# The first sum of a unit's weight blocks, made by an accumulating transfer in place of a VectorE addition, in the input projection of a hybrid retention and recurrence layer

## The chip, the cores and the metric

The kernel runs on one core of a Trainium2 chip. The metric is the device time of one execution in microseconds (us), less is better. Engines: TensorE (PE, matmuls), VectorE (DVE), ScalarE (ACT), GpSimd (POOL) and SyncE (SP, which issues most of the DMA transfers).

## The reference, cut to what matters

One layer over 1024 positions and 1024 channels, all in float32. The stage of this case is the combined input projection, whose 8192 columns are q and k, v, the swish gate, the two branches of the recurrence and the two merge gates.

```
h = rms_norm(x, norm1_w[l])
proj = h @ w_in[l]
q, k, v, g_ret, x_lru, y_lru, gate_ret, gate_lru = jnp.split(proj, SPLIT_POINTS, axis=-1)
...
x = x + mix @ w_out[l]
h = rms_norm(x, norm2_w[l])
up = h @ ffn_w_up[l]
...
```

## The kernel before, in words

**Tiles and products.** Every large product is taken by a fast scheme of the Strassen-Winograd kind: a unit of 256 output columns and 1024 positions is made of seven products of blocks in place of eight. A unit's weights (the A side) are four blocks of 128x512 float32, A11, A12, A21 and A22, 256 KB each, loaded from DRAM into tiles of the pool `w` (22 tiles). From them come seven operands, in the order `PRODS` (line 528): A11, S1 = A21 + A22, S2 = S1 - A11, A12, S3 = A21 - A11, A22, S4 = A12 - S2. Each operand is split into a rounded high part and a rest, which are two more `w` tiles: a cast on ScalarE (line 597) and a subtraction on VectorE (line 598). PE then runs 12 matmuls of 128x128 by 128x512 to a product (line 848): four slices of the contraction, with three of the four combinations of high and rest. The B side (positions) is split once and kept in the pool `u`.

**Who calls what.** `loads()` (line 635) issues a unit's block loads on SyncE in the job's own order (line 649). `prep_fast()` (line 673) makes the operands: S1 by a VectorE addition into a new tile (line 683), S2 in that same tile (line 686), S4 in the same tile again (line 689), S3 in the tile of A11 (line 692). `mm_fast()` (line 826) issues the products. `pump()` (line 727) lets preparation run up to seven finished operands ahead of PE (`NBLK`) and loads up to six blocks ahead of preparation (`AHEAD`).

**The input projection.** 24 units go through this (`add`, line 1763). The order is `SEQ` (line 549): merge gates, the recurrence's branches, and four retention heads of two units each, with the recurrence, the retention and the sums for later stages running beside them as generators that `advance()` takes in turn. v's columns are made ahead of it by a routine of their own, `values()`. The other stages that use the same helpers (both branch outputs, the output projection, the feed-forward part) have 48 more units.

**What sets the order.** The program is built twice. `Plan` reads the first build, gives every instruction a duration and every transfer a time to landing from its own table, ranks all instructions by when they are due, and forms an order for each engine. 150 drafts, made by random shifts around the waits that its own model shows, are tried and the best is kept; the second build is held to it. So each engine's queue is fixed, and a changed instruction anywhere lets all of it be drawn anew. Engines meet by semaphores only. SyncE, GpSimd and ScalarE each issue their transfers in their fixed order, and an instruction that waits holds up all that stands behind it on its engine.

**GpSimd before.** In this stage it copies the rotary tables (lines 1182 to 1185, eight transfers) and raises the variances of the retention's groups to -1/2 (line 1410, eight times, 128x4). Later it issues the stores to `ff_d` (line 1941).

Of the kernel before, what the change touches and what calls it, by code (L numbers as in the profile page):

```python
# [16 lines left out]
ALU = mybir.AluOpType  # L17
# [73 lines left out]
IN_RATE = 1.5  # L91
# [436 lines left out]
PRODS = ("A11", "S1", "S2", "A12", "S3", "A22", "S4")  # L528
# [25 lines left out]
def tile_trunk_layer(ctx, tc, x, xt, front, positions, params, consts, normf, w_in, w_v, w_ro, w_lo,  # L554
                     w_out, w_up, w_dn, w_gate, out):
    nc = tc.nc
    V, S, G, PE, SY = nc.vector, nc.scalar, nc.gpsimd, nc.tensor, nc.sync
# [36 lines left out]
    def split(src, get=get):  # L594

        hi, lo = get(F32R), get(F32R)
        S.copy(hi, src)  # L597
        V.tensor_sub(lo, src, hi.bitcast(F32))  # L598
        return hi, lo
# [10 lines left out]
    class Job:  # L610
        def __init__(self, src, op, emit, post=None, fast=False, last=False, drop12=False,
                     pre=None, fetch=None, order=None, ready=None, by=None, rate=RATE, mate=False,
                     prods=PRODS, stage=None, halves=()):
            self.pre, self.ready, self.by, self.rate = pre, ready, by, rate
            self.stage, self.halves = stage, halves
            self.mate, self.prods = mate, prods
            self.order = order or (("A11", "A21", "A22", "A12") if fast else ORD_T)
            self.fetch, self.got = fetch, {}
            self.src, self.op, self.emit, self.post = src, op, emit, post
            self.fast, self.last, self.drop12 = fast, last, drop12  # L620
            self.raw, self.blk = {}, {}
# [13 lines left out]
    def loads():  # L635
        i = 0
        while True:
            while i >= len(queue):
                yield None
            group = queue[i:i + 1 + queue[i].mate]  # L640
            while group[0].stage and not state["open"]:
                yield None
            for nm in () if group[0].stage else group[0].order:
                m, kh = int(nm[1]) - 1, int(nm[2]) - 1
                for jb in group:
                    while jb.ready is not None and not jb.ready(m, kh):
                        yield None
                    t = W.get()
                    SY.dma_start(t, jb.src(m, kh))
                    jb.raw[nm] = t  # L650
                    state["raws"] += 1
                    yield True
            i += len(group)

    def raw(jb, nm):
        while nm not in jb.raw:
            if next(state["load"]) is None:
                yield None
        return jb.raw[nm]

    def done(jb, *names):
        for nm in names:
            W.put(jb.raw[nm], late=SOONER)
            state["raws"] -= 1
# [7 lines left out]

    def prep_fast(jb):
        uses = {"A11": {"A11", "S2", "S3"}, "A21": {"S1", "S3"}, "A22": {"S1", "A22"}, "A12": {"A12", "S4"}}
        s = None
        for nm in PREP.get(jb.prods, jb.prods):
            for r in uses:
                if nm in uses[r]:
                    yield from raw(jb, r)
            r = jb.raw  # L680
            if nm == "S1":
                src = s = W.get()
                V.tensor_add(s, r["A21"], r["A22"])  # L683
            elif nm == "S2":
                src = s
                V.tensor_sub(s, s, r["A11"])  # L686
            elif nm == "S4":
                src = s
                V.tensor_sub(s, r["A12"], s)  # L689
            elif nm == "S3":  # L690
                src = r["A11"] if uses["A11"] == {"S3"} else W.get()
                V.tensor_sub(src, r["A21"], r["A11"])  # L692
            else:
                src = r[nm]
            jb.blk[nm] = split(src, W.get)
            state["blocks"] += 1
            if nm == "S4" or nm == "S3" and src is not r["A11"]:
                W.put(src, late=SOONER)
            for k, u in uses.items():
                if nm in u:  # L700
                    u.remove(nm)
                    if not u:
                        done(jb, k)
            yield True

    def preps():
        i = 0
        while True:
# [14 lines left out]
            i += len(group)  # L723

    state["load"], state["prep"] = loads(), preps()

    def pump(force=None):
# [226 lines left out]
    def pair_src(w, i):  # L954
        return lambda m, kh: w[i, 2 * m + kh]
# [101 lines left out]
    h1 = {}  # L1057
# [703 lines left out]
    jobs = []  # L1761

    def add(i, emit, post=None):
        jobs.append(Job(pair_src(w_in, i), h1, emit, post, fast=True, rate=IN_RATE))

    gates = [(w, n) for n in range(4) for w in range(2)]

    def add_gate():
        w, n = gates.pop(0)
        add(16 + 4 * w + n, emit_gate(w, n))  # L1770

    for what in SEQ.split():
        if what == "v":
            jobs.append(Job(None, h1, None, stage=values))
        elif what == "g":
            add_gate()
        elif what[0] == "y":
            n = int(what[1])
            add(2 * n + 1, emit_y(n))
        elif what[0] == "x":  # L1780
            n = int(what[1])
            add(2 * n, emit_to(xl, None, True), lambda n=n: lru_block(n, dict(xl)))
        else:
            hd = int(what[1])
            base = 8 + 2 * hd

            def head(hd=hd):
                mine = dict(qk)
                return chain(rotary_head(hd, mine), retention_head(hd, mine))
            add(base, emit_to(qk), head)  # L1790
            add(base + 1, emit_to(gg, AF.Silu, True), lambda hd=hd: chain(
                ret_out(hd, dict(gg)), *(four_sums(*(og_d, to_d) if hd > 1 else (w_out, tw_d), 2 * (hd % 2) + j)
                                         for j in range(2))))
# [312 lines left out]
    def down_post(g, t):  # L2106
        def fn():
# [3 lines left out]
            if g == 1 and t == 3:  # L2111
# [5 lines left out]
                 prods=ENDING if (g, t) == (2, 3) else PRODS,  # L2117
                 halves=(slice(0, TH // 2), slice(TH // 2, TH)) if (g, t) == (2, 3) else (),
# [72 lines left out]
```

## Time and profile before

| | us |
|---|---|
| median of 3 runs | 1567.7 (1567.51 to 1568.17) |
| the profiled execution | 1566.78 |
| its span, first to last instruction | 1565.0 |
| PE busy in the span | 1557.1 |
| VectorE, ScalarE, GpSimd busy | 1343.9, 952.5, 61.0 |

The columns of an instruction group are: line, engine, operation, output<-inputs by tile names without buffer numbers, shapes, xcount | busy us, mean ns of one | the engine's idle time just before them, and what ended it. A row of waits reads: who waited for whom, us in total, times, longest. A row of the timeline reads: start, duration, engine, line, operation, tiles; in brackets the idle time before it. "q" behind an engine's name is its sequencer, which issues the DMAs. A matmul's mean of 391 ns is longer than the distance of two starts, since matmuls are pipelined.

### The profile page before, as it was taken

To read this page: it belongs to the slowest core of one execution; us is meant where nothing else is said; L and a number is where in the kernel's file an instruction comes from. 1 tells how busy PE (TensorE), PEld (TensorE's weight loads), DVE (VectorE), ACT (ScalarE), POOL (GpSimd) and SP (SyncE) were. 2 spreads that over 40 slices of the span, in tenths; PEclk is the share of its full clock that TensorE was granted. 3 is DMA by queue.
4 is the path that set the end of the run, shared out by engine and by line. 5 is a ranking of instruction groups with operands and counts; after the bars stand their busy time and mean duration, and the time that the engine had idled before them with its cause. 6 is when DMAs were issued, how large, how long until landed. Compare 5 with 4: busy or idle time off the path is not lost.

```text
span 1565.0 us, 21570 instructions
## 1 busy us (share of the span) xinstructions
PE 1557.1 (99%) x7057; PEld 1290.7 (82%) x7057; DVE 1343.9 (86%) x2397; ACT 952.5 (61%) x1675; POOL 61.0 (4%) x81
## 2 busy tenths in 40 slices
PE   9999999999999999999999999999999999999998
PEld 7888888888888888888888888888888888888887
DVE  8999988998899988999998899777777778887875
ACT  8558766766568777855456665455454547554653
POOL 0001000000000000000000001000000000000000
PEclk9999999999999999999999999999999999999999
DMA  9344334454364346875995336444444476777752
GB/s 328 121 139 130 115 129 124 140 187 155 114 203 142 101 135 186 266 276 174 315 315 173 106 115 223 141 135 142 134 138 144 146 239 196 250 266 256 265 187 80
DMA packets 157713, 278.97 MB, mean 178 GB/s; under 512 B 17048, under 2 KB 29728, under 8 KB 157600
## 3 DMA queue, kind: packets, MB, share of 16 engines
q1 hardware_dynamic: 152080, 261.79, 51.3%
q0 software_dynamic: 4224, 13.64, 2.7%
q10 hardware_dynamic: 1296, 2.17, 0.4%
q8 instruction: 55, 0.90, 0.2%
q14 instruction: 58, 0.48, 0.1%
HBM read 192.59 MB, written 83.89 MB: 177 GB/s over the span
## 4 chain that ended last, share of the span: by engine, by line
PE 93%; DMA 3%; DVE 2%; ACT 1%; issue 1%; SPq 0%; POOLq 0%; POOL 0%; DVEq 0%; ACTq 0%
PE g L848 81%; PE g L1606 5%; PE a L1257 3%; DMA w<-mix_d 1%; PE a L1382 1%; PE a L1380 1%; DMA u<-tw_d 1%; PE a L1392 1%; DVE w L598 0%; PE a L1884 0%; PE a L1372 0%; PE a L1451 0%; DMA w<-w_lo 0%; DMA sg_d<-u 0%; DVE u L598 0%
## 5 line engine op out<-in xcount | busy, mean ns | idle before, releaser
L848 PE MATMUL g<-u,w 128*128 128x512 f32 x6060 | 1412.6, 391 | 0.0
L848 PEld LDWEIGHTS g<-u,w 128*128 128x128 f32 x6060 | 1129.7, 188 | 229.0
L597 ACT CAST w<-w 128x512 fp32r<-128x512 f32 x519 | 319.0, 621 | 334.4 <-PE g L848 240.3
L598 DVE TENSOR_TENSOR w<-w,w 128x512 fp32r<-128x512 f32 x519 | 352.9, 684 | 84.4 <-ACT w L597 81.0
L597 ACT CAST u<-u 128x512 fp32r<-128x512 f32 x253 | 151.2, 619 | 60.6 <-DVE u L1239 7.5
L598 DVE TENSOR_TENSOR u<-u,u 128x512 fp32r<-128x512 f32 x253 | 166.7, 682 | 4.3 <-ACT u L597 4.0
L900 ACT COPY u<-g 128x512 f32<-128x512 f32 x148 | 86.4, 583 | 61.3 <-PE g L848 58.4
L877 DVE TENSOR_TENSOR u<-g,u 128x512 f32<-128x512 f32 x146 | 100.1, 686 | 22.1 <-PE g L848 16.8
L1936 DVE SCALAR_TENSOR_TENSOR u<-u,par,u 128x511 f32<-128x511 f32 (+1 forms) x96 | 71.6, 746 | 12.8 <-ACT u L1933 12.2
L1606 PE MATMUL g<-w,u 128*128 128x512 f32 x252 | 58.7, 389 | 0.0
L1606 PEld LDWEIGHTS g<-w,u 128*128 128x128 f32 x252 | 47.2, 188 | 9.9
L1941 POOL DMA_DIRECT2D ff_d<-u x48 | 36.2, 754 | 444.6 <-DVE u L1940 434.2
L683 DVE TENSOR_TENSOR w<-w,w 128x512 f32<-128x512 f32 x72 | 49.2, 683 | 2.7 <-DMA w<-ff_d 1.4
L897 ACT COPY g<-g 128x512 f32<-128x512 f32 x70 | 40.4, 577 | 17.8 <-PE g L848 17.6
L1257 PE MATMUL a<-u,u 128*128 128x512 f32 x192 | 50.4, 390 | 0.5 <-ACT u L597 0.5
L686 DVE TENSOR_TENSOR w<-w,w 128x512 f32<-128x512 f32 x72 | 49.3, 684 | 0.7
L689 DVE TENSOR_TENSOR w<-w,w 128x512 f32<-128x512 f32 x72 | 49.2, 683 | 0.3 <-DMA w<-w_lo 0.2
L692 DVE TENSOR_TENSOR w<-w,w 128x512 f32<-128x512 f32 x72 | 49.2, 683 | 0.4
L1933 ACT ACTIVATE u<-u,par 128x512 f32<-128x512 f32 x48 | 39.1, 816 | 7.8 <-DVE u L877 7.0
L1257 PEld LDWEIGHTS a<-u,u 128*128 128x128 f32 x192 | 35.9, 188 | 8.6 <-ACT u L597 1.3
L871 DVE TENSOR_TENSOR u<-u,u 128x512 f32<-128x512 f32 x34 | 23.2, 687 | 20.5 <-ACT u L900 20.4
L1940 DVE TENSOR_TENSOR u<-u,u 128x512 f32<-128x512 f32 x48 | 32.9, 687 | 5.4 <-ACT u L1939 5.4
(216 smaller groups left out, 1158.8 us busy)
## 6 DMA issues: line engine op xcount, KB each, us to landing
w<-w_in SPq DMA_DIRECT2D x96, 256.0 KB, 2.8
w<-w_up SPq DMA_DIRECT2D x96, 256.0 KB, 2.7
u<-w_dn SPq DMA_DIRECT2D x84, 256.0 KB, 3.2
u<-x_d SPq DMA_DIRECT2D x52, 256.0 KB, 4.4
x_d<-u SPq DMA_DIRECT2D x48, 256.0 KB, 3.6
ff_d<-u POOLq DMA_DIRECT2D x48, 256.0 KB, 2.9
td_d<-u SPq DMA_DIRECT2D x48, 256.0 KB, 3.0
u<-td_d SPq DMA_DIRECT2D x48, 256.0 KB, 4.5
```

The costliest lines, as they stand in the source:

```text
L597: S.copy(hi, src)
L598: V.tensor_sub(lo, src, hi.bitcast(F32))
L683: V.tensor_add(s, r["A21"], r["A22"])
L686: V.tensor_sub(s, s, r["A11"])
L689: V.tensor_sub(s, r["A12"], s)
L692: V.tensor_sub(src, r["A21"], r["A11"])
L848: PE.matmul(bank[:, s], w[a][:, c], need(op, (SETS[nm], j))[b][:, s], start=first and n == 0, stop=n == 11, skip_group_check=True)
L877: V.tensor_add(u, bank, u)
L900: S.copy(u, bank)
L1257: PE.matmul(ps, wg[g][a][:, cs], xs[k][b], start=q == 0, stop=q == 5)
L1606: PE.matmul(bank, o[p][:, c], w[q], start=first and j == n == 0, stop=j == 3 and n == 2, skip_group_check=True)
L1936: V.scalar_tensor_tensor(c[:, s:], src[:, :TH - s], w, c[:, s:], ALU.mult, ALU.add)
```

## The change

In the 24 units of the input projection the load order gets a fifth entry, S1. For it the block A21 is loaded into a `w` tile by SyncE, and then GpSimd issues a transfer of A22 from DRAM that adds onto that tile. That tile is S1; the VectorE addition is gone. A21 and A22 are loaded once more, for S3 and for A22 itself. The order of a unit's loads is A11, S1, A12, A21, A22 in place of A11, A21, A22, A12. The tile of S1 is now one that a load filled, and it is given back with the other loaded blocks. The other stages keep the addition.

```
+            if summed:
+                self.order = "A11", "S1", "A12", "A21", "A22"
...
             for nm in () if group[0].stage else group[0].order:
-                m, kh = int(nm[1]) - 1, int(nm[2]) - 1
+                m, kh = (1, 0) if nm == "S1" else (int(nm[1]) - 1, int(nm[2]) - 1)
                 for jb in group:
...
                     t = W.get()
                     SY.dma_start(t, jb.src(m, kh))
+                    if nm == "S1":
+                        G.dma_start(t, jb.src(1, 1), accum_op=ALU.add)
                     jb.raw[nm] = t
...
         uses = {"A11": {"A11", "S2", "S3"}, "A21": {"S1", "S3"}, "A22": {"S1", "A22"}, "A12": {"A12", "S4"}}
+        if "S1" in jb.order:
+            uses["A21"], uses["A22"], uses["S1"] = {"S3"}, {"A22"}, {"S1", "S2", "S4"}
...
-            if nm == "S1":
+            if nm == "S1" and nm in r:
+                src = s = r[nm]
+            elif nm == "S1":
                 src = s = W.get()
                 V.tensor_add(s, r["A21"], r["A22"])
...
-            if nm == "S4" or nm == "S3" and src is not r["A11"]:
+            if nm == "S4" and "S1" not in r or nm == "S3" and src is not r["A11"]:
...
-        jobs.append(Job(pair_src(w_in, i), h1, emit, post, fast=True, rate=IN_RATE))
+        jobs.append(Job(pair_src(w_in, i), h1, emit, post, fast=True, rate=IN_RATE, summed=True))
```

Lines behind the edits move by up to 8 in the changed kernel: 649 becomes 651 for the loads, the accumulating transfer is 653, 1410 becomes 1418.

Place 1 is SyncE in the unit of the second retention head's q and k (its blocks have the numbers from 423 on) and the start of the next unit (from 461 on). Before, A22 is w_429, A21 w_423, A12 w_436, and w_437 is the next unit's A11:

```order
L649 DMA w_429_2282<-w_in 128x512
L649 DMA w_423_2264<-w_in 128x512
L649 DMA w_436_2303<-w_in 128x512
L649 DMA w_437_2307<-w_in 128x512
L1344 DMA u_447_2582<-v_d 128x512
L1344 DMA u_454_2631<-v_d 128x512
L649 DMA w_467_2448<-w_in 128x512
L649 DMA w_461_2430<-w_in 128x512
```

Now, where w_423 is the tile of S1, w_422 is A11, w_429 A12, and w_436 and w_437 are the second loads of A21 and A22:

```order
L651 DMA w_429_2291<-w_in 128x512
L651 DMA w_422_2266<-w_in 128x512
L651 DMA w_423_2272<-w_in 128x512
L651 DMA w_436_2312<-w_in 128x512
L651 DMA w_437_2316<-w_in 128x512
L1352 DMA u_447_2590<-v_d 128x512
L1352 DMA u_454_2639<-v_d 128x512
L651 DMA w_460_2425<-w_in 128x512
```

A unit has one load more, and the load that S1 needs stands third in its group. On GpSimd, from the rotary copies on, there stood before:

```order
L1183 DMA u_298_1267<-u_288_1031 64x512
L1182 DMA u_298_1267<-u_288_1031 64x512
L1410 TENSOR_TENSOR rs<-rs,half 128x4 x8
L1859 TENSOR_TENSOR nst<-nst,half 128x2 x4
L1941 DMA ff_d<-u_1898_9565 128x4x128
```

Now, with w_423 and w_461 of the units above among them:

```order
L653 DMA w_385_2127<-w_in 128x512
L653 DMA w_423_2272<-w_in 128x512
L653 DMA w_461_2439<-w_in 128x512
L1418 TENSOR_TENSOR rs<-rs,half 128x4 x2
L653 DMA w_499_2814<-w_in 128x512
L653 DMA w_537_3041<-w_in 128x512
L1418 TENSOR_TENSOR rs<-rs,half 128x4 x2
L653 DMA w_575_3437<-w_in 128x512
L653 DMA w_613_3643<-w_in 128x512
```

The row scales of the retention stand behind accumulating transfers, each of which waits for its tile's load.

Place 2 is ScalarE in the same unit. Before, the first cast here is A11's, and the second is that of the sum w_444, which VectorE had made:

```order
L597 CAST w_440_2321<-w_399_2165 128x512
L597 CAST w_445_2341<-w_444_2339 128x512
L1318 COPY u_422_2368<-u_416_2223 64x512
L1317 COPY u_422_2368<-u_416_2223 64x512
L1337 ACTIVATE u_431_2476<-a_53_2471,kdr 128x128 x3
L597 CAST sm_8_2540<-sm_7_2538 128x128
L1337 ACTIVATE u_431_2476<-a_53_2471,kdr 128x128
L597 CAST u_432_2481<-u_431_2476 128x512
L1387 COPY u_441_2548<-a_57_2544 128x256
```

Now the second cast reads w_423, the tile onto which the transfer adds:

```order
L597 CAST w_440_2330<-w_422_2266 128x512
L597 CAST w_444_2348<-w_423_2272 128x512
L1326 COPY u_422_2375<-u_416_2229 64x512
L1325 COPY u_422_2375<-u_416_2229 64x512
L1345 ACTIVATE u_431_2486<-a_53_2481,kdr 128x128 x3
L597 CAST sm_8_2548<-sm_7_2546 128x128
L1345 ACTIVATE u_431_2486<-a_53_2481,kdr 128x128
L597 CAST u_432_2491<-u_431_2486 128x512
L597 CAST w_452_2395<-w_429_2291 128x512
L1395 COPY u_441_2556<-a_57_2552 128x256
```

The cast keeps its place among its neighbours, and waits there for a transfer in place of VectorE.

More of the change, by code (lines that the diff above doesn't have):

```diff
@@ L612, in __init__ @@
                      pre=None, fetch=None, order=None, ready=None, by=None, rate=RATE, mate=False,
-                     prods=PRODS, stage=None, halves=()):
+                     prods=PRODS, stage=None, halves=(), summed=False):
             self.pre, self.ready, self.by, self.rate = pre, ready, by, rate
```

## The prediction

> **What bounds the kernel now.** I read the page first, for what each engine does, and then the windows, for the stage that the change edits.
>
> ```profile
> span 1565.0 us, 21570 instructions
> ...
> PE 1557.1 (99%) x7057; PEld 1290.7 (82%) x7057; DVE 1343.9 (86%) x2397; ACT 952.5 (61%) x1675; POOL 61.0 (4%) x81
> ...
> PE 93%; DMA 3%; DVE 2%; ACT 1%; issue 1%; SPq 0%; POOLq 0%; POOL 0%; DVEq 0%; ACTq 0%
> ```
>
> TensorE (PE) is busy for 1557.1 of 1565.0 us and is 93% of the chain that ended last. VectorE (DVE), from which the change takes work, is busy for 86% and is 2% of that chain. The input projection's units have PE from about 88 us to 637 us. The windows give busy time by engine, the granted clock, the share of the DMA engines and GB/s:
>
> ```profile
> core 0: us, PE busy (x) PEld busy (x) DVE busy (x) ACT busy (x) POOL busy (x), PEclk, DMA share, GB/s
> ...
> 240.00:455.00 215.00, 214.94 (x1099) 181.39 (x1098) 193.25 (x412) 134.30 (x279) 9.22 (x8) 1.00 0.49 156
> 88.00:637.00 549.00, 548.45 (x2578) 457.19 (x2578) 497.06 (x964) 384.90 (x664) 13.54 (x16) 1.00 0.45 143
> 754.00:834.00 80.00, 79.85 (x355) 65.89 (x354) 75.70 (x129) 45.96 (x88) 1.11 (x2) 1.00 0.95 322
> ```
>
> In this stage PE idles for 549.00 - 548.45 = 0.55 us in all, at the full granted clock. VectorE idles for 52 us, ScalarE (ACT) for 164 us, GpSimd (POOL) nearly always, and the DMA engines are 45% used. So VectorE is dense, but it is ahead of PE. Nearly all of the 0.55 us is one wait, shown by the groups of this window and by its timeline:
>
> ```profile
> L1257 PE MATMUL a<-u,u 128*128 128x512 f32 x192 | 50.4, 390 | 0.5 <-ACT u L597 0.5
> ...
> 171.44 0.62 ACT L597 CAST u<-u 128x512 fp32r<-128x512 f32 x1 [1.26 <-DMA sg_d<-u]
> ```
>
> It is a gate matmul that waits for a cast, which itself had waited for a store to sg_d. It isn't a weight block.
>
> **The change part by part.** (1) Removed: 24 additions of two blocks, one to a unit.
>
> ```profile
> L683 DVE TENSOR_TENSOR w<-w,w 128x512 f32<-128x512 f32 x72 | 49.2, 683 | 2.7 <-DMA w<-ff_d 1.4 <-DMA w<-mix_d 1.2
> ...
> ACT w L597 <- DVE w L683: 4.5, 4, 2.9
> ```
>
> The 72 are those of all the stages; 24 of them go: 24 x 0.683 = 16.4 us of VectorE. ScalarE waited for such an addition four times in this stage, for 4.5 us together, and PE didn't notice it. The gain on the path can't exceed the 0.55 us that PE idles, and the wait that makes up most of it is not for an addition. I book 0 to -0.55 us, and take -0.2.
>
> (2) Added loads. SyncE issues five loads to a unit in place of four, and GpSimd one accumulating transfer:
>
> ```profile
> L649 SPq DMA_DIRECT2D w<-w_in x87: 327/333/1062, 95.0 to 593.9; - x87
> ...
> DMA to landing us min/median/max: 2.4/2.7/5.7
> ...
> q1 hardware_dynamic: 152080, 261.79, 51.3%
> ```
>
> 24 x 0.333 = 8.0 us more of SyncE's issuing, over 549 us. In engine time, q1 moved 261.79 MB in 0.513 x 1565 = 803 us of all sixteen engines, so a block of 256 KB (0.262 MB) costs 0.80 us. There are 48 more transfers, and the 24 accumulating ones read their destination besides: 72 x 0.80 = 58 us, or 0.10 of the stage, which brings its share from 0.45 to 0.55 (0.59 in the densest window). In the window from 754 us the share is 0.95 and PE still has 79.85 of 80 us. On the path: 0.
>
> (3) The accumulating transfer itself. The trace has none. Its nearest rows are the stores that GpSimd issues, of the same size, and its group for their issue:
>
> ```profile
> ff_d<-u POOLq DMA_DIRECT2D x48, 256.0 KB, 2.9
> ...
> L1941 POOL DMA_DIRECT2D ff_d<-u x48 | 36.2, 754 | 444.6 <-DVE u L1940 434.2 <-DVE u L1982 10.4
> ```
>
> From below: 2.9 us from issue to landing, no faster than a plain copy. From above: 5.8 us, as if the destination were read by a full transfer of its own before the other one. I take the lower end, 2.9 us, the row that it is nearest to, and keep 5.8 for the range. GpSimd gets 24 x 0.754 = 18.1 us, beside 13.54 us in the stage.
>
> The Trainium skill, "Collectives: The Full Stack", section "The bandwidth ceiling: the fold count and why AG ≠ RS ≠ AR", speaks against a price of a plain copy: a transfer that adds reads two sources through one ring and so moves at half the rate, while the addition takes no time. By that rule, an estimate, one more 0.80 us makes it 3.7 us; the forecast would be the same and the margin below smaller, and no run here shows it yet.
>
> (4) The new chain. Before, both blocks are loaded side by side and then added: 2.7 + 0.68 = 3.4 us after the later load's issue. After, the accumulating transfer waits on GpSimd until the first load has landed: 2.7 + 2.9 = 5.6 us (2.7 + 5.8 = 8.5 at the upper end). What covers this is the lead. Each product is 12 matmuls:
>
> ```profile
> 637.31 116.52 PE g L848 x514
> ```
>
> That is 0.227 us for one, 2.72 us for a product and 19.0 us for a unit's seven. The code keeps up to seven finished blocks ahead of PE (NBLK) and six loaded ones (AHEAD): 6/4 of a unit, 28.6 us, before, and 6/5, 22.9 us, with five loads to a unit. The accumulation falls within that. The narrower limit is the place of the cast on ScalarE, which runs in order. For the unit whose rows the change's section shows, the timeline gives:
>
> ```profile
> 220.96 5.77 SPq L649 DMA_DIRECT2D w<-w_in  x3
> ...
> 225.74 0.69 DVE L683 TENSOR_TENSOR w<-w,w 128x512 f32<-128x512 f32 x1
> ...
> 228.52 1.22 ACT L597 CAST w<-w 128x512 fp32r<-128x512 f32 x2
> ```
>
> The later of the two loads is issued at 220.96, the addition runs at 225.74, and its result is cast by the second of the two casts, 228.52 + 0.60 = 229.1 us. If the load and the cast keep these places, the accumulating transfer may take 229.1 - 220.96 - 2.7 = 5.4 us before the cast is late. It has 2.5 us to spare at 2.9 us. On the path: 0. If that cover goes, the cast waits, and behind it on ScalarE stand the keys' scalings (L1337), a score's cast and the copy that frees an "a" bank (L1387), for which PE's retention matmuls wait.
>
> (5) Waits on GpSimd. The retention's eight row scales (L1410) now stand behind accumulating transfers that wait for loads:
>
> ```profile
> L1410 POOL TENSOR_TENSOR rs<-rs,half x8: 1007/1008/1479, 251.4 to 433.6; 128x4 f32<-128x4 f32 x8
> ...
> ACT u L1414 <- DVE rs L1411: 3.8, 3, 1.3
> ```
>
> One of them can be late by a load and an issue, 2.7 + 0.75 = 3.5 us. The normalised outputs go on to transposes that the code puts behind a pause (ret_out), so I book 0.
>
> (6) The redrawn plan. The order of all engines is drawn again. PE's changes in few places, VectorE's and ScalarE's in many, and ScalarE gets 53 table loads in place of 47:
>
> ```profile
> L1468 ACT ACT_TABLE_LOAD x11 | 14.1, 1283 | 0.2
> ```
>
> 6 x 1.283 = 7.7 us on an engine that idles for 612 us of the span. On the path: 0, with a spread of about 1 us either way, twice the stage's whole idle time.
>
> Sum: -0.2 us on the profiled execution, which took 1566.78 us with its span of 1565.0 (1.8 us lie around it): 1566.6. The three runs have a median of 1567.7, which is 0.9 above it, so I predict 1567.5 us.
>
> **The rivals.** A, slower: the accumulating transfer lands late. It decides from 5.4 us on. At the upper bound, 5.8 us, each of the 24 casts is 0.4 us late; if ScalarE's idle time absorbs none of it, 24 x 0.4 = 9.6 us, 1577 us. For it: no row here shows such a transfer, and ScalarE and VectorE run in a fixed order. Against: ScalarE idles for 164 us in the stage, 6.8 us a unit, and PE uses a block several products after its cast.
>
> B, slower: GpSimd's queue. If half of eight row scales are 3.5 us late and PE's transposes wait for them, 4 x 3.5 = 14 us, 1582 us. Against: GpSimd waits for VectorE there, and ScalarE waited for the result three times, 1.3 us at most.
>
> C, the redrawn plan puts a wait where none was, most likely where the DMA engines are at 0.95: a late landing of 2.7 us twice, 1573 us; or it takes away half of the 7.3 us that PE idles outside of the stage (7.9 - 0.55), 3.7 us, 1564 us.
>
> D, faster: VectorE's 16.4 us were what held the stage back, in a way that the busy time of a pipelined PE hides. The time would be down to 1551 us if all of it were on the path; the stage's windows leave 0.55.
>
> **How the numbers follow.** A measurement of this kernel can tell about 0.2%, 3.1 us, from no change. Chances: the forecast 0.74, with its own range of 1566 to 1569.5; A 0.14; B 0.03; C 0.04 slower and 0.03 faster; D 0.02. Faster is 0.03 + 0.02 = 0.05, same 0.74, slower 0.14 + 0.03 + 0.04 = 0.21. The range reaches from 1565.5, a little below the forecast's own, up to 1574, which takes in C's slower case and the milder half of A (two thirds of its 9.6 us); some 0.15 is left out.
>
> **What would show it.** Right: DVE loses some 16 us in the stage and PE still idles under 1 us there; the accumulating transfer's median issue to landing is under 5.4 us; the casts of w wait no longer for VectorE or DMA than now. Wrong: ScalarE's waits list the accumulating transfer (DMA w<-w_in) with tens of us, and PE waits for ACT or DVE between 88 and 637 us; or PE's waits stand at the transposes behind L1414 (B); or PE's idle time changes outside of the stage (C); or the stage gets shorter by more than 0.55 us (D).

## The result and the profile after

| | before | after |
|---|---|---|
| median of the runs side by side | 1567.94 us (13 runs, 1566.59 to 1569.67) | 1571.34 us (13 runs, 1569.76 to 1573.94) |
| ratio, with its 95% interval | | 1.0025 [1.0018, 1.0033] |
| the profiled execution | 1566.78 us, span 1565.0 | 1570.95 us, span 1569.2 |

The changed kernel is slower by 3.4 us, 0.25%, a little more than the 0.2% that a measurement of this kernel can tell. One profiled execution of the experiments, that of the first kernel there, was disturbed (8842 us) and is left out. Lines below the edits in the program stand 8 lines further down: the cast is still L597, but a unit's matmuls are now L856 (L848), the retention matmuls L1388 (L1380), the keys' scalings L1345 (L1337), the gate matmuls L1265 (L1257). The accumulating transfer is L653, the loads L651.

First the page of the changed kernel, the same lines as before:

```profile
span 1569.2 us, 21673 instructions
...
PE 1558.6 (99%) x7057; PEld 1290.5 (82%) x7057; DVE 1331.1 (85%) x2373; ACT 958.7 (61%) x1681; POOL 82.4 (5%) x105
...
PE 96%; DMA 2%; ACT 2%; issue 0%; DVE 0%; SPq 0%; POOLq 0%; POOL 0%; ACTq 0%; DVEq 0%
```

VectorE did lose its work (1343.9 to 1331.1 us), and ScalarE has grown on the chain that ended last. Then the windows of the changed kernel, with the columns as in the prediction (length, busy time by engine, granted clock, DMA share, GB/s):

```profile
240.00:455.00 215.00, 213.53 (x1091) 179.74 (x1090) 185.87 (x402) 132.36 (x277) 16.49 (x17) 1.00 0.56 170
88.00:637.00 549.00, 546.27 (x2564) 454.17 (x2563) 482.37 (x938) 389.34 (x665) 33.19 (x39) 1.00 0.55 164
754.00:834.00 80.00, 79.69 (x352) 65.70 (x351) 76.00 (x126) 44.97 (x85) 0.00 (x0) 1.00 0.94 317
```

In the stage VectorE is busy 14.7 us less (497.06 to 482.37), GpSimd 19.7 us more, and the DMA share is 0.55, from 0.45. But PE now idles for 549.00 - 546.27 = 2.73 us, where it idled for 0.55. That is 2.2 of the 4.2 us by which this profiled span is longer than the one before. The waits of the changed kernel in this stage (engine, what waited for what: us in total, times, longest) name the places:

```profile
ACT w L597 <- DMA w<-w_in: 11.6, 5, 3.5
...
PE a L1388 <- ACT u L1345: 1.4, 1, 1.4
PE a L1265 <- ACT u L597: 1.3, 1, 1.3
```

ScalarE's casts wait for a block in transfer, and PE waits twice for ScalarE. The wait at L1265 is the one that was there before (0.5 us), a cast behind a store to sg_d. It has grown by 0.8 us, but its matmul starts no later than before, since PE came to it sooner. The first row is the kernel before:

```profile
172.12 0.73 PE L1257 MATMUL a<-u,u 128*128 128x512 f32 x2 [0.49 <-ACT u L597]
...
171.94 0.73 PE L1265 MATMUL a<-u,u 128*128 128x512 f32 x2 [1.26 <-ACT u L597]
```

The wait at L1388 is new. The chain that ended last shows what released it (start, us, what):

```profile
272.58 4.25 DMA w<-w_in
276.85 0.04 POOLq L653
...
277.39 6.79 DMA w<-w_in
...
284.26 0.09 ACT w L597
...
285.41 0.62 ACT u L1326
286.04 0.03 ACT u L1345
...
287.06 0.37 ACT u L1345
287.42 0.18 ACT sm L597
287.61 0.27 ACT u L1345
...
288.70 0.39 PE a L1388
```

Read it from the top: the load of A21 takes 4.25 us to land, the accumulating transfer onto it 6.79, then comes the cast of the sum, and behind that on ScalarE the cast of a block of v, a keys' chain and a score's cast, for which a retention matmul waits. It is one unit, the third head's q and k. Units are numbered from 0 by their columns, and this one is number 12 of the 24; it is the eleventh to be taken. The timeline gives the same place with each wait in brackets:

```profile
277.39 0.91 POOL L653 DMA_DIRECT2D w<-w_in  x1 [7.11 <-DMA w<-w_in]
...
284.26 0.62 ACT L597 CAST w<-w 128x512 fp32r<-128x512 f32 x1 [2.56 <-DMA w<-w_in]
...
288.70 0.39 PE L1388 MATMUL a<-u,sm 128*128 128x256 f32 x1 [1.41 <-ACT u L1345]
```

And the accumulating transfers as a group, their issue on GpSimd (ns, min/median/max) and their time to landing:

```profile
L653 POOL DMA_DIRECT2D w<-w_in x24: 854/866/1107, 72.1 to 588.8; - x24
...
DMA to landing us min/median/max: 3.9/4.5/6.8
```

### The profile page after: what moved, and what is told of

It is laid out like the page before. It is cut to its first block, busy times and chain, and to the rows that moved or that the text cites. A ratio compares the mean times of both kernels' runs of the same rounds, so it can differ in the third digit from the quotient of the medians.

```text
span 1569.2 us, 21673 instructions
## 1 busy us (share of the span) xinstructions
PE 1558.6 (99%) x7057; PEld 1290.5 (82%) x7057; DVE 1331.1 (85%) x2373; ACT 958.7 (61%) x1681; POOL 82.4 (5%) x105
## 4 chain that ended last, share of the span: by engine, by line
PE 96%; DMA 2%; ACT 2%; issue 0%; DVE 0%; SPq 0%; POOLq 0%; POOL 0%; ACTq 0%; DVEq 0%
PE g L856 84%; PE g L1614 5%; PE a L1265 3%; PE a L1390 1%; PE a L1388 1%; DMA w<-w_in 1%; PE a L1400 1%; PE a L1892 0%; PE a L1380 0%; PE a L1459 0%; DMA w<-mix_d 0%; DMA sg_d<-u 0%; DMA u<-w_out 0%; PE g L1649 0%; PE g L1666 0%
## 5 line engine op out<-in xcount | busy, mean ns | idle before, releaser
L856 PE MATMUL g<-u,w 128*128 128x512 f32 x6060 | 1412.3, 391 | 0.3 <-ACT u L908 0.3
L856 PEld LDWEIGHTS g<-u,w 128*128 128x128 f32 x6060 | 1129.9, 188 | 229.5 <-ACT u L908 1.0
L597 ACT CAST w<-w 128x512 fp32r<-128x512 f32 x519 | 318.3, 621 | 323.6 <-PE g L856 217.9
L597 ACT CAST u<-u 128x512 fp32r<-128x512 f32 x253 | 151.0, 620 | 66.0 <-DVE u L1247 7.8
L908 ACT COPY u<-g 128x512 f32<-128x512 f32 x148 | 86.0, 581 | 67.5 <-PE g L856 64.2
L1265 PE MATMUL a<-u,u 128*128 128x512 f32 x192 | 50.3, 392 | 1.3 <-ACT u L597 1.3
L694 DVE TENSOR_TENSOR w<-w,w 128x512 f32<-128x512 f32 x72 | 49.3, 685 | 0.6
L905 ACT COPY g<-g 128x512 f32<-128x512 f32 x70 | 40.5, 578 | 14.7 <-PE g L856 14.7
L700 DVE TENSOR_TENSOR w<-w,w 128x512 f32<-128x512 f32 x72 | 49.2, 683 | 0.3
L697 DVE TENSOR_TENSOR w<-w,w 128x512 f32<-128x512 f32 x72 | 49.1, 684 | 0.2
L1265 PEld LDWEIGHTS a<-u,u 128*128 128x128 f32 x192 | 35.5, 188 | 10.2 <-ACT u L597 2.6
L653 POOL DMA_DIRECT2D w<-w_in x24 | 21.6, 901 | 384.1 <-PE g L856 108.7
L879 DVE TENSOR_TENSOR u<-u,u 128x512 f32<-128x512 f32 x34 | 23.1, 688 | 19.9 <-ACT u L908 19.8
L1212 ACT COPY u<-g 128x512 f32<-128x512 f32 x56 | 32.6, 582 | 10.6 <-PE g L856 10.6
```

The lines of the kernel that those rows point to most:

```text
L856: PE.matmul(bank[:, s], w[a][:, c], need(op, (SETS[nm], j))[b][:, s], start=first and n == 0, stop=n == 11, skip_group_check=True)
L905: S.copy(y, bank)
L908: S.copy(u, bank)
L1265: PE.matmul(ps, wg[g][a][:, cs], xs[k][b], start=q == 0, stop=q == 5)
```

## The experiments

Two theories stood at the start. The late landing: an accumulating transfer lands late enough, somewhere, to make a cast late that PE's work stands behind. The redrawn plan: the orders of all engines were drawn again, and any redraw costs or gains about this much. In the expectations these are L and R; T is a third, that the 48 added transfers and GpSimd's queue cost it. Only with the last two kernels T and S mean what is said there. The kernel before ran beside each kernel, on the same chip; its medians in the three sets of runs were 1567.51, 1567.78 and 1567.71 us, and each ratio is to the one of its set. Where the difference of two kernels has an interval, it comes from their 11 runs each, drawn again with replacement.

**All transfers plain, orders the same.** One argument goes; the sum of A21 and A22 is then not made, and A22 overwrites A21.

```
-G.dma_start(t, jb.src(1, 1), accum_op=ALU.add)
+G.dma_start(t, jb.src(1, 1))
```

> The changed kernel with every engine's order as it is, but GpSimd's transfer of A22 replaces the tile's content in place of adding onto it (the sum is left out). Theory L (the accumulating transfer takes 4.5 us to land where a plain one takes 2.9, so that ScalarE's cast of S1 is late and holds up what stands behind it): the landing falls to about 2.9 us, PE's wait at the retention's score matmul near 288 us (1.4 us) goes, and the time falls by 1.5 to 3 us, to about 1569. Theory R (the redrawn order as such costs the 3.4 us): same order, so 1571 as before the edit, within 0.7 us. Theory T (the 48 more transfers and GpSimd's queue cost it): 1571 too.

It took 1568.66 us (10 runs), a ratio of 1.0007 [0.9998, 1.0016]. The same kernel again, for its profile:

> The kernel of the plain transfers once more (the sum is left out), for a profile and a comparison on the same chip. Theory L (late landing): 1.5 to 3.5 us below the changed kernel, landing 2.8 to 3.2 us, no PE wait over 0.5 us between 240 and 455 us. Theories R (the redrawn order) and T (traffic and GpSimd's queue): within 0.7 us of the changed kernel.

1568.67 us, 1.0004 [0.9995, 1.0013]. Its transfers as a group and the stage's window:

```profile
L653 POOL DMA_DIRECT2D w<-w_in x24: 538/538/737, 72.3 to 587.0; - x24
...
DMA to landing us min/median/max: 2.7/3.3/5.4
```

```profile
88.00:637.00 549.00, 548.13 (x2573) 456.14 (x2573) 484.65 (x941) 391.37 (x669) 25.54 (x39) 1.00 0.51 165
```

Same orders, the same loads, the same chain from load to GpSimd's transfer to cast; only the adding is gone. The transfer lands 1.1 to 1.2 us earlier (3.3 us, a little over what was expected, for 4.4 and 4.5 us) and GpSimd issues it in 0.538 in place of 0.866 us. PE idles for 0.87 us in the stage, and the kernel is 2.3 us faster [1.3, 3.1] than the changed one of the same set (below). What the plan alone and the added loads alone can cost is what this kernel still has above the kernel before, 0.9 us.

**The changed kernel again**, beside it:

> The changed kernel as it is, so that the following three are compared with it on one chip. All theories: 1570.5 to 1572, the accumulating transfers' median landing near 4.5 us, and PE's wait at the retention's score matmul near 288 us in its profile.

1570.98 us, 1.0019 [1.0010, 1.0028]. The result stands. In this execution the wait at L1388 was longer, and something follows it. The waits, and the windows of 4 us from 288 us on:

```profile
PE a L1388 <- ACT u L1345: 2.1, 1, 2.1
```

```profile
288.00:292.00 4.00, 3.27 (x11) 2.79 (x12) 3.65 (x6) 3.90 (x9) 0.00 (x0) 0.62 0.00 0
292.00:296.00 4.00, 4.00 (x22) 3.42 (x21) 3.32 (x8) 1.44 (x4) 0.00 (x0) 0.96 0.01 3
```

The granted clock (third number from the right) falls to 0.62 behind the wait: PE finishes 11 matmuls in a window in which the first profile after has 16. If the clock alone set PE's pace, the loss would be 4 x 0.38 + 4 x 0.04 = 1.7 us, on top of 2.1 us of waiting; the starts of the matmuls, in the last section, give 1.2 us. In the first profile after, with 1.4 us of waiting, the clock stayed at 1.00.

**The planner told of the transfer's real size.** The planner's table had plain values for GpSimd's transfers; here it gets the measured issue and 1.7 us more to landing, and draws the orders again. The computation is the change's.

```
+self.adds = self.eng == "Pool" and self.read and self.bytes == 4 * P * TH
-self.hold = 750.0 if self.eng == "Pool" else 330.0
+self.hold = 870.0 if self.adds else 750.0 if self.eng == "Pool" else 330.0
...
+ 1700.0 * s.adds
```

> The changed kernel with the planner told that an accumulating transfer takes 0.87 us to issue and 1.7 us longer to land, so that it draws the order with a later cast of S1. Theory L: ScalarE's waits for w_in fall from 12.8 us to under 5 us, no PE wait over 0.5 us between 240 and 455 us, and 1568 to 1569.5 us. Theory R: another draw, anywhere from 1567 to 1572, with no tie to ScalarE's waits for w_in. Theory T: 1571.

1568.66 us, 1.0007 [0.9998, 1.0016]: the accumulating transfers are all there, and the cost can't be told from none (1.15 us are left by the medians). The first fence has their issue and landing, the second ScalarE's waits for blocks (each line is one further down here):

```profile
L654 POOL DMA_DIRECT2D w<-w_in x24: 854/864/1109, 73.2 to 587.3; - x24
...
DMA to landing us min/median/max: 3.7/4.3/7.4
```

```profile
ACT w L598 <- DMA w<-w_in: 5.4, 3, 2.5
```

They land hardly earlier, one even after 7.4 us, and that of unit 12 after 7.2. ScalarE's casts wait for 5.4 us in place of 11.6, a little over the 5 expected, and PE idles for 549.00 - 548.66 = 0.34 us in the stage. So a transfer this late need not hold PE up where the order leaves room for it. It is one draw, which differs in other places too.

**Other plans.** The planner's random seed alone, for the kernel before and for the changed one.

```
-RandomState(1)
+RandomState(2)
...
-RandomState(1)
+RandomState(3)
```

> The kernel before with another seed for the planner's random shifts: what a new draw of the order alone does. Theory L: within 1.5 us of the kernel before, since before has no late landing to be exposed. Theory R: it differs from the kernel before by 2 to 4 us, as the change did. Theory T: no change, 0 to 1 us.

> The changed kernel with the same other seed. Theory L: 1569 to 1573, by how many casts of S1 the draw puts within 4.5 us of their transfer; the time goes with ScalarE's waits for w_in. Theory R: differs from the changed kernel by 2 to 4 us without them. Theory T: 1571, within 0.7 us.

> The kernel before with another seed of the planner's search and nothing else changed: all orders are drawn again. The theory that a redrawn plan is worth up to about 1 us either way: 1567.0 to 1569.0 us, beside 1568.7 from another seed. If it gives under 1567.0 or over 1569.5, plans scatter more than that, and the 1 us left over in the changed kernel needs no other cause.

The kernel before took 1568.68 us with seed 2 (1.0009 [1.0000, 1.0018]) and 1567.77 with seed 3 (1.0001 [0.9992, 1.0010]): a redraw alone is worth 0.1 to 1.2 us here. The changed kernel with seed 2 took 1570.51 (1.0017 [1.0008, 1.0026]). A retention matmul is late there too, but not behind a sum:

```profile
ACT w L597 <- DMA w<-w_in: 6.8, 4, 3.0
...
PE a L1388 <- ACT u L597: 1.7, 1, 1.7
...
335.31 0.62 ACT L597 CAST u<-u 128x512 fp32r<-128x512 f32 x1 [3.70 <-DMA u<-v_d]
```

The matmul starts at 339.99, in the fourth head. The cast ahead of it that waited, the last row, reads a block of v. Its load landed 6.9 us after its issue, beside the accumulating transfer of that unit, which took 6.9 us as well and for whose sum no cast stood waiting. So a late landing among many transfers shows with this seed too, but that the adding causes it is not shown here: no run has this order with plain transfers.

**Plain in eight units.** Units 8 to 15 get a plain transfer, the other 16 accumulate; the orders are the same, and the sums of those eight are left out.

```
-G.dma_start(t, jb.src(1, 1), accum_op=ALU.add)
+G.dma_start(t, jb.src(1, 1), **({} if jb.plain else {"accum_op": ALU.add}))
...
+jobs[-1].plain = 8 <= i < 16
```

> The changed kernel, every engine's order as it is, with plain transfers in the eight units of the retention heads alone (their sums are left out) and accumulating ones in the other sixteen. Theory L with its place at the heads, where matmuls of the retention wait for what stands behind the cast: it gains most of what the plain kernel gains, 1.3 to 2.5 us below the changed kernel. If the lateness costs in all units alike: a third, 0.8 us. R and T: within 0.7 us of the changed kernel.

1569.59 us, 1.0011 [1.0002, 1.0020]: 1.4 us [0.4, 2.4] of the 2.3 go with a third of the units. That is more than the 0.8 of an even spread, but the interval doesn't exclude it.

**A dearer accumulating transfer.** The same bytes, with every 2 KB row cut into four pieces of 512 B out of the unit's four blocks (another sum than A21 + A22, of the same size).

```
-G.dma_start(t, jb.src(1, 1), accum_op=ALU.add)
+G.dma_start(t.rearrange("p (b c) -> p b c", b=4), jb.strips, accum_op=ALU.add)
...
+jobs[-1].strips = w_in[i][:, :, 0:P].rearrange("b p c -> p b c")
```

> The changed kernel, every engine's order as it is, whose accumulating transfer reads as many bytes in pieces of 512 B, a quarter of each of the unit's four blocks (another sum than the kernel needs). It should be slower to issue and to land, 6 to 9 us by guess. Theory L: the time rises with it and more than in proportion, since one cast after another comes late: 1578 to 1610, and ScalarE's waits for w_in reach 40 us or more. R: 1571. T: up to 2 us more, for GpSimd's issuing.

1576.12 us, 1.0051 [1.0036, 1.0065], in 5 runs. The direction is the late landing's, but its numbers were missed: the time is below 1578 us, the landing's median is 5.1 us, short of the 6 to 9 expected, and the casts' waits came nowhere near 40 us. The transfers, PE's waits, and the windows behind the wait:

```profile
L653 POOL DMA_DIRECT2D w<-w_in x24: 1274/1290/1483, 72.2 to 595.9; - x24
...
DMA to landing us min/median/max: 4.3/5.1/9.6
```

```profile
PE a L1388 <- ACT u L1345: 2.9, 1, 2.9
PE a L1265 <- ACT u L597: 2.3, 2, 1.3
```

```profile
292.00:296.00 4.00, 2.88 (x9) 2.56 (x10) 3.71 (x7) 3.90 (x9) 0.00 (x0) 0.55 0.00 0
296.00:300.00 4.00, 4.00 (x14) 3.23 (x13) 2.44 (x6) 1.69 (x5) 0.00 (x0) 0.59 0.00 0
```

Its longest landing, 9.6 us, is that of unit 12 again. PE waits 2.9 us and then has the clock at 0.55 and 0.59. The wait ends at 293.1, so the lower clock would cost 2.9 x 0.45 + 4 x 0.41 = 2.9 us more if it alone set PE's pace. By the starts it is 2.3 us up to the next pair of L1380: from L1388 there it takes 298.83 - 293.12 = 5.71 us, and 290.48 - 287.11 = 3.37 in the plain kernel, which has the same matmuls in the same order. The plain kernel waits 0.4 us here too. So this place gives 2.9 - 0.4 + 2.3 = 4.8 of the 7.45 us that the kernel lies above the plain one. The waits at L1265, 2.3 us for 0.5, are a second place.

**One unit alone.** The sharp test, with the same edit as for eight units: unit 12 plain and the others accumulating (`i == 12`), and its complement (`i != 12`). Orders the same; the sums of the plain units are left out.

> The changed kernel, with a plain transfer in place of the accumulating one in one unit only, the third head's q and k (number 12 of 24; the sum of its blocks is left out, so its products are others); the order of all engines is the same. Theory T (one late cast holds the path: the sum of this unit lands late, the cast waits, and behind it the key scalings that a retention matmul waits for): that matmul waits under 0.5 us, where it waited 1.4 and 2.1 us, the granted clock stays at 1.00 behind it, and the time is 1569.3 us (1568.7 to 1570.2), near the kernel with all transfers plain (1568.7). Rival S (the cost is spread over all the sums' landings): a 24th of 2.5 us, 0.1 us, goes, and the time stays at 1571.0 (1570.4 to 1571.6).

> The complement: the transfer is accumulating in that one unit only, and plain in the other 23 (their sums are left out); orders the same. Theory T: the matmul still waits over 1 us, and the time is 1570.3 us (1569.5 to 1571.3). Theory T is weakened if the wait stays but the time falls to 1568.7. Rival S: the wait is under 0.5 us and the time is 1568.8 (1568.2 to 1569.4). A third case, in which the transfer lands late only beside other accumulating transfers (contention): it lands in about 5 us in place of 6.8 and the time is 1568.8 as well.

With unit 12 alone made plain: 1569.04 us (1.0011 [1.0002, 1.0020]), 1.9 us [0.4, 2.2] under the changed kernel. With unit 12 alone accumulating: 1570.24 us (1.0015 [1.0006, 1.0024]), 1.6 us [0.5, 2.5] above all plain. Both medians are within what theory T expected and outside of what S did. Either interval alone reaches down to what S allows, 0.6 and 0.7 us; that both lie this way, and the waits, decide for T. (The profiled execution with unit 12 plain is the slowest of its 11, 1571.47 us: the waits are read from it, the time is not.) The waits of PE in the two, first with unit 12 plain, then with it alone accumulating:

```profile
PE a L1340 <- DVE u L1329: 0.5, 1, 0.5
PE a L1388 <- ACT u L597: 0.3, 1, 0.3
PE a L1265 <- ACT u L597: 0.3, 1, 0.3
```

```profile
PE a L1388 <- ACT u L1345: 1.5, 1, 1.5
PE a L1265 <- ACT u L597: 0.5, 1, 0.5
```

The complement's timeline has the transfer, which lands 7.2 us after its issue, and the cast:

```profile
276.12 0.95 POOL L653 DMA_DIRECT2D w<-w_in  x1 [6.79 <-DMA w<-w_in]
...
283.36 0.62 ACT L597 CAST w<-w 128x512 fp32r<-128x512 f32 x1 [2.63 <-DVE w L598]
```

The transfer landed at 276.12 + 7.2 = 283.3, and a VectorE subtraction for another block ended at the same moment, which the profile names as the releaser; with all transfers plain the cast started at 282.65. The third case, that contention with other accumulating transfers makes it late, falls: it lands late although the 23 others are plain. Even plain it takes 5.4 us there, against a median of 3.3, since that stretch is full of transfers (below). In the run with unit 12 plain another unit's sum landed after as much as 8.3 us, and no wait of PE in the stage was above 0.5 us. It is the place that counts.

What this place has are DMA engines that were busy throughout already before the change. The DMA share is the second number from the right (a transfer counts whole where it starts, so it can pass 1), first before and then after:

```profile
272.00:280.00 8.00, 8.00 (x41) 6.60 (x40) 7.49 (x14) 6.04 (x12) 0.00 (x0) 1.00 0.96 324
...
272.00:280.00 8.00, 8.00 (x41) 6.61 (x40) 8.00 (x14) 5.64 (x12) 0.91 (x1) 1.00 1.02 355
```

And the sum isn't alone in being late. ScalarE's next cast behind it reads a block of v, whose load (L1344, now L1352) is issued at 276.6 before and at 277.0 after. Its time to landing, before and after:

```profile
DMA to landing us min/median/max: 4.1/4.1/4.1
...
DMA to landing us min/median/max: 7.0/7.0/7.0
```

It lands at 284.0, the sum at 284.2, and v's cast starts at 284.78. With the sum in time and v's load as it is, that cast could have started some 0.7 us earlier and no more. Beside a plain transfer in unit 12 the load of v took 5.3 to 6.8 us, beside an accumulating one 7.0 to 7.3. So the two kernels above show what the accumulating transfer costs in this unit; how much of it comes by its own cast, and how much by the v load that it shares the DMA engines with, they don't tell apart.

All runs with the same orders, at that one place (landing of unit 12's transfer, wait of its cast, wait of the retention matmul, granted clock in the 4 us window in which or behind which it ends):

| kernel | landing, us | cast waits | PE waits | clock | median, us |
|---|---|---|---|---|---|
| all plain | 5.4 | 1.5 | 0.4 | 1.00 | 1568.7 |
| plain in unit 12 | 5.5 | 1.2 | under 0.1 | 1.00 | 1569.0 |
| plain in units 8 to 15 | 5.9 | 2.0 | 0.8 | 1.00 | 1569.6 |
| accumulating in unit 12 alone | 7.2 | 2.6 | 1.5 | 1.00 | 1570.2 |
| changed kernel | 6.8 | 2.6 | 1.4 | 1.00 | 1571.3 |
| changed kernel again | 7.0 | 3.2 | 2.1 | 0.62 | 1571.0 |
| pieces of 512 B | 9.6 | 4.1 | 2.9 | 0.55 | 1576.1 |

By and large the cast's wait, and with it PE's, grows with this one landing, though the profiled execution is a single one and the median is over all.

## Why the prediction was wrong, point by point

The forecast was no change, 1567.5 us with 1566 to 1569.5 as its own range; the kernel took 1571.3. The wider range, up to 1574, takes that in, but only by way of the rivals. What came is rival A's mechanism, in one place in place of twenty-four, and there with a second late transfer beside the sum's. Of the signs named ahead, the median landing (4.5 us) stood on the side of right, and PE's 2.73 us of idle time and ScalarE's 11.6 us of waits for blocks on the side of wrong.

**What bounds the kernel** was read rightly: PE, with 0.55 us to spare in the stage. (1) 14.7 us left VectorE there and none of it reached the path; rival D falls. (2) The DMA share rose to 0.55 and to 0.56 in the densest window (0.55 and 0.59 forecast). But the 0 on the path rests on averages over 215 and 549 us. In the 8 us from 272 us on the share was 0.96 before and is 1.02, and the load of v there lands after 7.0 us in place of 4.1. The 0.95 from 754 us on, where PE lost little, says nothing about a stretch in which ScalarE's casts wait for what is in transfer.

**(3), the transfer's size, was mis-sized.** I took "the lower end, 2.9 us, the row that it is nearest to". It measured 4.5 us (3.9 to 6.8) from issue to landing. A plain transfer by GpSimd at the same places takes 3.3, so the adding is worth 1.1 to 1.2 us of it, and the other 0.4 lie between a store to ff_d and a load here. Between the bounds of 2.9 and 5.8 the middle would have been the better choice, since no row of a transfer that reads its destination was there. The rule of the Trainium skill, "Collectives: The Full Stack", section "The bandwidth ceiling: the fold count and why AG ≠ RS ≠ AR", which that page gives for the reduce step of a ring collective, pointed the right way: by it 2.9 became 3.7, an estimate with 0.8 us added, and the runs show 1.1 to 1.2. GpSimd's issue took 0.866 us in place of 0.754.

**(4), the cover, is the step that failed.** It named the right chain: the cast of the sum, behind it the keys' scalings and a score's cast, and then PE's retention matmuls. But the spare time was worked out for a single unit, the second head's q and k, with a median load of 2.7 us, and then taken for all: "the accumulating transfer may take 229.1 - 220.96 - 2.7 = 5.4 us". In unit 12 the load took 4.25 and the transfer 6.79, 11.0 us together, where 8.1 were allowed for by the second head's unit and 5.6 forecast; and between the sum's cast and the keys' scalings stands a cast of v there, whose load was late as well. The median of 4.5 us is below the 5.4 from which rival A was to decide, and A happened all the same, because a median says nothing about the one unit that stands in the densest stretch. The wait of PE there, 1.4 to 2.1 us (0.4 with plain transfers), was priced at 0.

**(5)** GpSimd's row scales cost nothing: ScalarE's waits for VectorE's part behind them were 1.1 and 0.8 us, within the 1.3 of before, and PE's list has no wait behind them. Rival B falls.

**(6), the redrawn plan**, "0, with a spread of about 1 us either way", is borne out: 0.1 and 1.2 us for two other seeds. Rival C in its slow form, a late landing where transfers are densest, is near to what happened, but the cause isn't the draw: with the same draw and plain transfers the wait is down to 0.4 us, and with the real size in the planner's table it is down to 0.2 with all sums accumulating.

The 3.4 us of the first set (3.2 in the later one) add up like this: about 1.9 from unit 12 (its wait and, in some executions, the lower clock behind it), 0.4 from the other 23 landings, and 0.9 that the kernel with plain transfers keeps above the kernel before. The complement puts the first two at 1.6 and 0.7, and the intervals are wide (0.4 to 2.2 and 0.5 to 2.5 for unit 12): that unit 12 is most of the adding's cost is likely, its exact share is not shown. The lower clock is rare: the granted clock over a whole execution of the changed kernel is 0.998 in 3 of 24, and 0.999 or more in the rest. For the 0.9 us the cause isn't settled: it is of the size of a redraw, but the 48 added transfers could have part in it, and no run has the added loads without a redraw. No version ran faster than the kernel before; with 0.55 us of PE idle in the stage there was nothing to win.

## What to carry to other kernels

A wait that every unit has must be priced at the unit with the least room, not at a typical one: take the slowest landing in the densest stretch against the cast's place there, as the chain of waits in unit 12 shows it (11.0 us where the median gave 5.6). An average of the DMA share over a stage hides the stretch that is full. When an operation moves to a transfer whose time no row shows, measure it and give the planner that time; here the measured issue and 1.7 us more to landing won back 2 to 3 us (1.0007 in place of 1.0019 to 1.0025), in the one draw that was run. And a gain on an engine that isn't late is no gain: 14.7 us of VectorE were worth nothing.

## What the runs showed of the hardware

An accumulating transfer of 256 KB from DRAM onto a block in SBUF, issued by GpSimd, took 4.3 to 4.5 us in the median from issue to landing where a plain one at the same places took 3.3, and 0.866 us of GpSimd's own time against 0.538. Cut into 512 B pieces it took 5.1 us to land and 1.29 us to issue.

The other finding is the clock. Waits of 1.4 and 1.5 us (and 1.7 with seed 2) left PE's granted clock at 1.00; a wait of 2.1 us was followed by 0.62 and one of 2.9 us by 0.55 and 0.59 in windows of 4 us. Within them the matmuls take longer. The plain kernel and the changed kernel's second run have the same matmuls in the same order, so the time from the one that waited to a later one can be compared (rows of the plain kernel first):

```profile
287.11 0.39 PE L1388 MATMUL a<-u,sm 128*128 128x256 f32 x1 [0.35 <-ACT u L1345]
...
292.39 0.51 PE L1400 MATMUL a<-u,u 128*128 128x256 f32 x3
```

```profile
288.73 0.43 PE L1388 MATMUL a<-u,sm 128*128 128x256 f32 x1 [2.06 <-ACT u L1345]
...
295.25 0.52 PE L1400 MATMUL a<-u,u 128*128 128x256 f32 x3
```

It is 292.39 - 287.11 = 5.28 us in the one and 295.25 - 288.73 = 6.52 us in the other. So in this execution a wait of 2.1 us cost 1.2 us more in lower clock, and the 2.9 us of the pieces 2.3 us or more. In windows of 2 us the clock is 0.73, 0.50 and 0.91 from 288 us on in the second run, and 0.61, 0.50, 0.50 and 0.69 from 292 us on with the pieces: it was halved for some 3.4 and 6.8 us. The Trainium skill, "TensorE: Matmul & The Clock Gate", section "What's actually happening", gives two clocks, half and full, and a monitor that looks at PE over windows of some 3.4 us that run freely. The halved clock agrees, and so do stretches of once and twice 3.4 us; that page's advice to avoid gaps above about 3 us ("Why this matters for your kernels") is too generous for this kernel, in which 2.1 us sufficed. One execution shows it; where between 1.7 and 2.1 us the limit lies, and whether it depends on where a wait falls, no run here tells.
